# Attention in a hybrid decoder block: the softmax sums of three of four query blocks go through DRAM, and the first block's scores stand in four slots in a row

## The chip, the cores and the metric

The kernel runs on one core of a Trainium2 chip. The metric is the device time of one execution in microseconds. Before the change the median of three runs was 2093.01 us (2092.22 to 2093.68). One further execution was profiled: it took 2091.41 us, of which 2089.6 us lie between its first and its last instruction (the span that all times inside the trace are counted in). The granted TensorE clock was 0.998 of full speed over the span.

## The reference, cut to what matters

The program is one decoder block over 2048 positions with a model width of 1024: a normed input projection, eight attention heads and a gated linear recurrence side by side, an output projection, and a gate at the end. The change touches the attention alone:

```
s = einsum('bhqd,bhkd->bhqk', qi, k) * scale
s = s + (ci[:, :, :, None] - c[:, :, None, :])       # c: cumulated log sigmoid of a forget logit
s = where(kpos[None, :] <= qpos[:, None], s, -inf)
w = softmax(s, axis=-1)
o = einsum('bhqk,bhkd->bhqd', w, v)
```

The softmax divides by a sum for each query. The kernel multiplies the finished output by the reciprocal of that sum, and it is this factor, one number for each of 512 queries, that has to reach every partition of a transposed output tile.

## The kernel before, in words

**Stages.** The first 1058 us are the projections and the recurrence, then comes the attention (1058 to 1608 us), then the output projection and the gate. Products are made in three parts by `mm3`, lines 67 to 69: high times high, high times low, low times high, in a four-byte type whose operands are split in two.

**Attention.** A unit is one head and one block g of 512 queries, g = 0 to 3. Because of the causal mask unit g meets 4g+4 blocks of 128 keys. The work of 32 units is written out by hand in slots, one slot for one key block of one unit; a head has 4+8+12+16 = 40 slots. They are counted here from 0 to 39 within a head: slots 0 to 3 are block 0, 4 to 11 block 1, 12 to 23 block 2, 24 to 39 block 3. `run_slot` writes what a slot issues, and this order is the order on each engine:

1. DMAs listed for the start of the slot (the list `before`), all on the queue of SP.
2. Score pieces (`piece`, lines 1219 to 1226): three matmuls into a bank `sbank` (three of them), then one VectorE instruction that adds the bias and mask, writes the row to `pr` and reduces a running minimum `m`.
3. The value products of the slot three earlier (`AHEAD` = 3, `add_values`), into `obank`.
4. At a unit's last value product, `finish_unit`: VectorE multiplies `obank` by the spread reciprocal `rb` to give `on`.
5. `turn_probs`: up to four TensorE transposes (line 1258) of 128x128 into a bank `tbank` (three of them), which ScalarE copies as the high part `th` (line 53) and VectorE completes with the low part `tl` (line 59). At a unit's second slot `spread_sums` follows (lines 1275 to 1279): each of the four columns of the reciprocals `r4` is repeated 128 times and transposed, so that one bank holds all 512 factors on all partitions, and ScalarE copies it to `rb`.
6. `gate_unit` on VectorE (`gs`), then the exponentials of score rows that became complete in this slot (ScalarE, line 1231, with a read of the accumulated sum), then chores listed for the slot's end (the list `after`): splits of the next head's keys and values (`kh`, `vh` on ScalarE, `kl`, `vl` on GpSimd), masks, and pieces of work for the recurrence and for later weights on GpSimd.

**Where the scores of a unit stand.** They are made during the unit before it, `LEAD` = 3 slots earlier than that unit's own slots. The table `s_at` spreads the 4g+4 pieces evenly: block 1 has two pieces in a slot (slots 37 to 0), block 2 three in two slots (1 to 8), block 3 four in three slots (9 to 20), and block 0 of the next head four pieces in sixteen slots, at slots 21, 25, 29 and 33. Its pieces have 128, 256, 384 and 512 keys, and each is a complete row, so that an exponential follows each.

Of the kernel before, what the change touches and what calls it, by code (L numbers as in the profile page):

```python
# [9 lines left out]
F32 = mybir.dt.float32  # L10
F32R = mybir.dt.float32r
AF = mybir.ActivationFunctionType
# [4 lines left out]
P = 128  # L17
S = 2048
D = 1024
NH = 8  # L20
# [52 lines left out]
def hymba_kernel(ctx: ExitStack, tc: tile.TileContext, x, xT, pT, w_p, w_v, w_o, w_ple, w_pg,  # L73
                 w_gates, vecs, rows, mgrp, out):
    nc = tc.nc
    const = ctx.enter_context(tc.tile_pool(name="const", bufs=1))
    dram = ctx.enter_context(tc.tile_pool(name="dram", bufs=1, space=DRAM))
# [14 lines left out]
    vo_d = dram.tile([2, 7, 2, P, 2 * WS], F32, name="vo_d")  # L92
    yl2_d = dram.tile([TB, P, D], F32, name="yl2_d")
    rl_d = dram.tile([1, S], F32, name="rl_d")
    wt_d = dram.tile([4, P, KD, 512], F32, name="wt_d")
    p2_d = dram.tile([2, 4, P, 512], F32, name="p2_d")
    p4_d = dram.tile([2, 4, P, 512], F32, name="p4_d")
# [17 lines left out]
    ident = const.tile([P, P], F32, name="ident")  # L115
# [45 lines left out]
    def pool_(stack, name, bufs=1, side="left", space=None):  # L161
        kw = {"side": side} if space is None else {"side": side, "space": space}
        return stack.enter_context(tc.tile_pool(name=name, bufs=bufs, reuse_waits="tile", **kw))
# [728 lines left out]
    for i in range(8):  # L892
        h, c = jobs.pop(0)
# [6 lines left out]
    for n in range(2):  # L900
# [6 lines left out]
        t = 139 + 6 * n  # L907
# [14 lines left out]
    for i in range(24):  # L922
        h, c = jobs.pop(0)
        t = VB + 11 + 5 * i
# [157 lines left out]
    for m, n in enumerate((0, "q0", 1, 2, "q1", 3, 4, 5, 6, 7)):  # L1082
        t = LWE + 1 + m
# [114 lines left out]
    av = pool_(p2, "av", 2)  # L1198
# [4 lines left out]
    psT = pool_(p2s, "psT", PS // 10 % 10, space=PSUM)  # L1203
# [49 lines left out]
    def turn_probs(g, u, sb):  # L1253

        q0 = max(0, sb - 4 * g)
        b = psT.tile([P, 512], F32, name="tbank")
        for i in range(q0, 4):
            nc.tensor.transpose(b[:, i * P:(i + 1) * P], u.P[i][:, sb * P:(sb + 1) * P], ident)  # L1258
        th = av.tile([P, 512], F32R, name="th", bufs=THB)
        tl = av.tile([P, 512], F32R, name="tl", bufs=THB)  # L1260
        n = slice(q0 * P, 512)
        split(nc, b[:, n], th[:, n], tl[:, n], "act", "dve")
        u.parts[sb] = (th, tl, n)

    def add_values(h, g, u, sb):
        s = heads[h]
        nsb = 4 * g + 4
        if sb == 0:
            u.o = psO.tile([P, 512], F32, name="obank")
        th, tl, n = u.parts.pop(sb)  # L1270
        mm3(nc, u.o[:, n], (s.vh[:, sb], s.vl[:, sb]), (th[:, n], tl[:, n]), sb == 0, sb == nsb - 1)

    def spread_sums(u):

        b = psT.tile([P, 512], F32, name="tbank")
        for i in range(4):
            nc.tensor.transpose(b[:, i * P:(i + 1) * P], u.r4[:, i:i + 1].broadcast_to([P, P]), ident)
        u.rb = av.tile([P, 512], F32, name="rb")
        nc.scalar.activation(u.rb, b, AF.Copy)

    def finish_unit(h, g, u):
        u.on = av.tile([P, 512], F32, name="on")
        nc.vector.tensor_tensor(out=u.on, in0=u.o, in1=u.rb, op=ALU.mult)

    def gate_unit(u):
        nc.vector.tensor_tensor(out=u.gs, in0=u.on, in1=u.gs, op=ALU.mult)

    def add_squares(h, g, u):
        on = u.on
        cs = slice(g * 512, (g + 1) * 512)  # L1290
        eng = nc.vector if (h, g) == (NH - 1, 3) else nc.gpsimd
        if h == 0:
            nc.gpsimd.tensor_tensor(out=acca[:, cs], in0=on, in1=on, op=ALU.mult)
        else:
            eng.tensor_tensor(out=on, in0=on, in1=on, op=ALU.mult)
            eng.tensor_tensor(out=acca[:, cs], in0=acca[:, cs], in1=on, op=ALU.add)
# [5 lines left out]
    def store_y(h, g, u):  # L1302
        nc.sync.dma_start(out=ya_d[h, :, g * 512:(g + 1) * 512], in_=u.gs)

    stages = [(h, g) for h in range(NH) for g in range(4)]
    NS = len(stages)
    t0, t = [], 4
# [4 lines left out]
    units = {0: u0}  # L1312
    before = {}
    after = {}

    def at(d, slot, f):
        d.setdefault(max(slot, 0), []).append(f)

    s_at = {}
    for n, (h, g) in enumerate(stages):  # L1320
        cnt = 4 * g + 4
        if n == 0:
            continue
        begin = max(t0[n - 1] - LEAD, 0)
        span = t0[n] - LEAD - begin
        for j in range(cnt):
            s_at.setdefault(begin + j * span // cnt, []).append((n, j))

    def begin_unit(n):
        h, g = stages[n]  # L1330
        u = units[n]
        u.parts = {}
        u.units = score_units(h, g, u)
# [98 lines left out]
    def run_slot(t, fill=None):  # L1432
        for f in before.pop(t, ()):
            f()
        post = []
        for n, j in s_at.pop(t, ()):
            if j == 0:
                begin_unit(n)
            f, a, z = units[n].units[j]
            e = f(a, z)  # L1440
            if e is not None:
                post.append(e)
        if fill is not None:
            fill()
        done = None
        if t - AHEAD in slots:
            n, sb = slots[t - AHEAD]
            h, g = stages[n]
            add_values(h, g, units[n], sb)
            if sb == 4 * g + 3:  # L1450
                done = units.pop(n)
                finish_unit(h, g, done)
                at(after, t + 3, lambda: add_squares(h, g, done))
                at(before, t + 4, lambda: store_y(h, g, done))
        if t in slots:
            n, sb = slots[t]
            turn_probs(stages[n][1], units[n], sb)
            if sb == 1:
                spread_sums(units[n])
        if done is not None:  # L1460
            gate_unit(done)
        for e in post:
            e()
        if t + 1 in t0[:NS]:
            r4 = units[t0.index(t + 1)].r4
            nc.vector.reciprocal(r4, r4)
        for f in after.pop(t, ()):
            f()
# [13 lines left out]
    for t in range(last_t0 + 1):  # L1482
        run_slot(t)
# [53 lines left out]
    def fill():  # L1537
        q, ks = fills.pop(0)
        products(q, ks, bank3)
        if ks[1] == KD - 1:  # L1540
            evict(q, av.tile([P, 512], F32, name="mx", tag="th", bufs=THB))
# [6 lines left out]
    for t in range(last_t0 + 1, end):  # L1548
        run_slot(t, fill if last_t0 + 3 <= t < last_t0 + 19 else None)
    for t in sorted(set(before) | set(after)):  # L1550
        run_slot(t)
# [359 lines left out]
```

## Time and profile before

| | |
|---|---|
| median of three runs | 2093.01 us |
| the profiled execution | 2091.41 us |
| its span | 2089.6 us |
| TensorE busy over the span | 99% |
| VectorE, ScalarE, GpSimd busy | 78%, 55%, 34% |
| attention, from the first transpose of probabilities to the last value product | 1058 to 1608 us |
| spread of the sums: transposes (line 1277) | 128, 19.2 us busy |
| spread of the sums: copies (line 1279) | 32, 18.9 us busy |

In the timelines below a row gives the start and the duration in us, the engine, the line, the operation, out<-in by the program's names, and in brackets the idle time of the engine before it with what ended it. Matmuls overlap: the recorded duration of one is longer than the distance to the start of the next, so costs on TensorE are read from starts. PEld is its weight load, SPq the queue on which SP issues DMAs.

### The profile page before, as it was taken

How to read it: one execution, taken by the hardware profiler on the slowest of the kernel's cores; microseconds unless marked ns; L12 is line 12 of the kernel's file. 1: busy time of each engine (PE TensorE's matmuls, PEld its weight loads, DVE VectorE, ACT ScalarE, POOL GpSimd, SP SyncE). 2: the span in 40 equal slices, each digit the busy share in tenths (PEclk: the TensorE clock that was granted, in tenths of full speed). 3: DMA queues.
4: the chain of work that ended last, by engine and by line, in shares of the span. 5: the costliest groups of instructions: out<-in, count | busy, mean ns of one | idle time of the engine just before them, and what ended most of it. 6: DMA issues, size and time to landing. Idle time of an engine off the chain costs nothing.

```text
span 2089.6 us, 31351 instructions
## 1 busy us (share of the span) xinstructions
PE 2062.3 (99%) x10586; PEld 1744.5 (83%) x10586; DVE 1625.5 (78%) x2706; ACT 1143.7 (55%) x1871; POOL 705.5 (34%) x613
## 2 busy tenths in 40 slices
PE   8999999999999999999999999999999999999999
PEld 6888888888988898888878888888888888888887
DVE  7976998696759877895588888888885778876665
ACT  7435765344337776664367777777773443452232
POOL 3434555332113335632035665666641000000000
PEclk9999999999999999999999999999999999999999
DMA  8698898987888898888657777777744887565553
GB/s 315 211 339 300 308 347 305 368 320 285 281 275 275 277 273 290 270 296 261 242 191 236 234 221 216 235 227 241 196 148 130 283 255 227 184 216 181 179 173 119
DMA packets 256976, 518.89 MB, mean 248 GB/s; under 512 B 25120, under 2 KB 91952, under 8 KB 256816
## 3 DMA queue, kind: packets, MB, share of 16 engines
q1 hardware_dynamic: 256672, 516.85, 75.2%
q8 instruction: 83, 1.36, 0.3%
q14 instruction: 77, 0.63, 0.1%
q10 hardware_dynamic: 144, 0.05, 0.0%
HBM read 314.55 MB, written 202.25 MB: 247 GB/s over the span
## 4 chain that ended last, share of the span: by engine, by line
PE 92%; DVE 4%; DMA 2%; ACT 1%; issue 1%; SPq 0%; DVEq 0%; ACTq 0%
PE bank L69 15%; PE bank L67 15%; PE bank L68 15%; PE pbank L69 7%; PE pbank L67 7%; PE pbank L68 7%; PE tbank L1258 5%; PE sbank L67 3%; PE sbank L69 3%; PE sbank L68 3%; PE obank L68 3%; PE obank L69 3%; PE obank L67 3%; DVE pr L1222 1%; PE bank L1780 1%
## 5 line engine op out<-in xcount | busy, mean ns | idle before, releaser
L67 PE MATMUL bank<-XH,op 128*128 128x512 f32 x876 | 342.3, 391 | 0.0
L69 PE MATMUL bank<-XH,op 128*128 128x512 f32 x876 | 340.9, 389 | 0.0
L68 PE MATMUL bank<-XL,op 128*128 128x512 f32 x876 | 340.8, 389 | 0.0
L357 DVE TENSOR_TENSOR c<-bank,c 128x512 f32<-128x512 f32 x280 | 186.7, 684 | 115.3 <-PE bank L69 103.0
L59 DVE TENSOR_TENSOR tl<-tbank,th 128x512 fp32r<-128x512 f32 (+1 forms) x320 | 192.3, 607 | 82.6 <-ACT th L53 79.8
L53 ACT ACTIVATE th<-tbank 128x512 fp32r<-128x512 f32 (+1 forms) x320 | 167.6, 530 | 117.5 <-PE tbank L1258 109.8
L68 PEld LDWEIGHTS bank<-XL,op 128*128 128x128 f32 x876 | 164.5, 188 | 34.5 <-issue 0.5
L69 PEld LDWEIGHTS bank<-XH,op 128*128 128x128 f32 x876 | 164.5, 188 | 34.3
L67 PEld LDWEIGHTS bank<-XH,op 128*128 128x128 f32 x876 | 164.5, 188 | 34.0 <-issue 0.5
L1231 ACT ACTIVATE pr<-pr,m 128x640 f32<-128x640 f32 (+7 forms) x124 | 152.0, 1226 | 45.0 <-DVE m L1222 44.3
L1258 PE MATMUL tbank<-ident,pr 128*128 128x128 f32 x1088 | 171.9, 273 | 0.0
L1258 PEld LDWEIGHTS tbank<-ident,pr 128*128 128x128 f32 x1088 | 134.1, 141 | 28.2 <-issue 0.2
L150 POOL TENSOR_TENSOR rsm<-rs,mhalf 128x1 f32<-128x1 f32 x16 | 8.7, 541 | 431.5 <-DVE rs L149 431.5
L67 PE MATMUL sbank<-kh,qh 128*128 128x512 f32 (+3 forms) x320 | 136.5, 427 | 5.1 <-DVE m L1222 3.7
L67 PE MATMUL obank<-th,vh 128*128 128x512 f32 (+1 forms) x320 | 123.2, 385 | 0.8 <-ACT th L53 0.8
L284 ACT ACTIVATE op<-wq 128x512 fp32r<-128x512 f32 (+1 forms) x96 | 60.0, 629 | 110.5 <-PE bank L69 73.0
L68 PE MATMUL obank<-tl,vh 128*128 128x512 f32 (+1 forms) x320 | 117.9, 368 | 1.2 <-DVE tl L59 1.1
L69 PE MATMUL sbank<-kh,ql 128*128 128x512 f32 (+3 forms) x320 | 116.7, 365 | 0.3 <-DVE ql L1162 0.2
L69 PE MATMUL obank<-th,vl 128*128 128x512 f32 (+1 forms) x320 | 116.8, 365 | 0.0
L68 PE MATMUL sbank<-kl,qh 128*128 128x512 f32 (+3 forms) x320 | 115.8, 362 | 0.0
L68 PE MATMUL bank<-op,XH 128*128 128x258 f32 x328 | 94.9, 289 | 2.8 <-DVE op L290 2.8
L69 PE MATMUL bank<-op,XL 128*128 128x258 f32 x328 | 95.9, 292 | 0.0
(327 smaller groups left out, 5755.9 us busy)
## 6 DMA issues: line engine op xcount, KB each, us to landing
wo_d<-op SPq DMA_DIRECT2D x140, 512.0 KB, 5.3
op<-wo_d SPq DMA_DIRECT2D x79, 512.0 KB, 5.4
wr<-wo_d SPq DMA_DIRECT2D x61, 512.0 KB, 5.4
wq<-in_w_p_dram SPq DMA_DIRECT2D x40, 512.0 KB, 6.2
vo_d<-op SPq DMA_DIRECT2D x28, 516.0 KB, 3.6
wst<-wt_d SPq DMA_DIRECT2D x56, 256.0 KB, 3.5
wst<-in_w_o_dram SPq DMA_DIRECT2D x40, 256.0 KB, 3.3
X<-xr_d SPq DMA_DIRECT2D x32, 257.5 KB, 4.0
```

The costliest lines, as they stand in the source:

```text
L53: nc.scalar.activation(hi, src, AF.Copy)
L59: eng.tensor_tensor(out=lo, in0=src, in1=f32(hi), op=ALU.subtract)
L67: nc.tensor.matmul(out, lhsT=wh, rhs=xh, start=start, stop=False)
L68: nc.tensor.matmul(out, lhsT=wh, rhs=xl, start=False, stop=False)
L69: nc.tensor.matmul(out, lhsT=wl, rhs=xh, start=False, stop=stop)
L150: nc.gpsimd.tensor_tensor(out=o, in0=t, in1=mhalf[:, :n], op=ALU.pow)
L284: nc.scalar.activation(op[:, :n], self.source(i, hf), AF.Copy)
L357: nc.vector.tensor_tensor(out=o, in0=x, in1=y, op=ALU.add)
L1222: nc.vector.tensor_tensor_reduce(out=pr[0][:, a:z], in0=b[:, :z - a], in1=u.dg[i][1] if z == L else u.bias[:, a:z], scale=-1.0, scalar=BIG ...
L1231: nc.scalar.activation(pr[0][:, :L], pr[0][:, :L], AF.Exp, bias=m2, scale=-1.0, accum_out=u.r4[:, i:i + 1])
L1258: nc.tensor.transpose(b[:, i * P:(i + 1) * P], u.P[i][:, sb * P:(sb + 1) * P], ident)
L1780: nc.tensor.transpose(b[:, k * P:(k + 1) * P], u.xt[:, kk * P:(kk + 1) * P], ident)
```

## The change

**Sums.** Blocks 1, 2 and 3 of a head (24 units) no longer use `spread_sums`. In the unit's second slot one transpose turns the 128x4 tile of reciprocals into 4x128, ScalarE copies these four rows to `rr`, two slots later SP stores them to DRAM as one row of 512, and another two slots later SP loads that row to all 128 partitions of `rb`. Block 0 keeps the four transposes.

**Scores.** For block 0 of heads 1 to 7 the span over which its four pieces are spread is 4 slots in place of 16: slots 21, 22, 23 and 24 of the head before.

```diff
+    rb_d = dram.tile([NH, 4, 512], F32, name="rb_d")
...
+    def turn_sums(u):
+        b = psT.tile([P, 512], F32, name="tbank")
+        nc.tensor.transpose(b[:4, :P], u.r4, ident)
+        u.rr = av.tile([P, P], F32, name="rr")
+        nc.scalar.activation(u.rr[:4], b[:4, :P], AF.Copy)
+
+    def store_sums(h, g, u):
+        nc.sync.dma_start(out=rb_d[h, g:g + 1, :].rearrange("o (t p) -> (o t) p", p=P), in_=u.rr[:4])
+
+    def load_sums(h, g, u):
+        u.rb = av.tile([P, 512], F32, name="rb")
+        nc.sync.dma_start(out=u.rb, in_=rb_d[h, g:g + 1, :].broadcast_to([P, 512]))
...
         begin = max(t0[n - 1] - LEAD, 0)
         span = t0[n] - LEAD - begin
+        if h > 0 and g == 0:
+            span = cnt
         for j in range(cnt):
             s_at.setdefault(begin + j * span // cnt, []).append((n, j))
...
             if sb == 1:
-                spread_sums(units[n])
+                h, g = stages[n]
+                u = units[n]
+                if g == 0:
+                    spread_sums(u)
+                else:
+                    turn_sums(u)
+                    at(before, t + 2, lambda: store_sums(h, g, u))
+                    at(before, t + 4, lambda: load_sums(h, g, u))
```

ScalarE in slots 20 to 27 of head 2, before. `pr` is a row of probabilities (its width tells which: 2048 is the last row of block 3, 128 to 512 are the rows of the next head's block 0), `th` the high part of a transposed block, `kh` the split of the next head's keys:

```order
L1231 ACTIVATE pr,r_12283<-pr,m 128x2048
L53 ACTIVATE th<-tbank 128x384
L1231 ACTIVATE pr,r_12586<-pr,m 128x128
L53 ACTIVATE th<-tbank 128x256
L53 ACTIVATE th<-tbank 128x128
L53 ACTIVATE th<-tbank 128x512 x2
L1279 ACTIVATE rb<-tbank 128x512
L1231 ACTIVATE pr,r_12586<-pr,m 128x256
L53 ACTIVATE th<-tbank 128x512
L53 ACTIVATE kh<-kvf 128x512
```

The same place on ScalarE now:

```order
L1232 ACTIVATE pr,r_12284<-pr,m 128x2048
L53 ACTIVATE th<-tbank 128x384
L1232 ACTIVATE pr,r_12587<-pr,m 128x128
L53 ACTIVATE th<-tbank 128x256
L1232 ACTIVATE pr,r_12587<-pr,m 128x256
L53 ACTIVATE th<-tbank 128x128
L1232 ACTIVATE pr,r_12587<-pr,m 128x384
L53 ACTIVATE th<-tbank 128x512
L1232 ACTIVATE pr,r_12587<-pr,m 128x512
L53 ACTIVATE th<-tbank 128x512
L1286 ACTIVATE rr<-tbank 4x128
L53 ACTIVATE th<-tbank 128x512
```

The exponentials of 256, 384 and 512 columns moved from slots 25, 29 and 33 to stand between the copies `th` of slots 22 to 25, and the copy of the spread sums became one of four rows.

SP's queue around slots 25 to 32 of head 2, before. `bias` and `dg` are the biases of the next head's block 1, `kvf` its keys and values (`kT_d`, `v_d`), `yl_d` a chore of the recurrence, `ya_d` the attention's output:

```order
L1394 DMA yl_d<-kvs 128x4x128
L1147 DMA bias<-nb_d 128x512
L1153 DMA dg_12734<-nb_d 128x256
L1153 DMA dg_12736<-nb_d 128x256
L1153 DMA dg_12738<-nb_d 128x384
L1153 DMA dg_12740<-nb_d 128x512
L1110 DMA kvf<-v_d 128x512
L1303 DMA ya_d<-gs 128x512
```

The same place on SP's queue now:

```order
L1410 DMA yl_d<-kvs 128x4x128
L1289 DMA rb_d<-rr 4x128
L1148 DMA bias<-nb_d 128x512
L1154 DMA dg_12749<-nb_d 128x256
L1154 DMA dg_12751<-nb_d 128x256
L1154 DMA dg_12753<-nb_d 128x384
L1154 DMA dg_12755<-nb_d 128x512
L1111 DMA kvf<-v_d 128x512
L1293 DMA rb<-rb_d 128x512
L1317 DMA ya_d<-gs 128x512
```

The store of the four rows stands ahead of the biases and the values, and the load of the row behind them, ahead of the output's store.

## The prediction

> **What bounds the kernel now.** I read the page first, then busy time by stretches of one head, then the chain of waits where it leaves TensorE.
>
> ```profile
> PE 2062.3 (99%) x10586; PEld 1744.5 (83%) x10586; DVE 1625.5 (78%) x2706; ACT 1143.7 (55%) x1871; POOL 705.5 (34%) x613
> ```
>
> ```profile
> 1197.90:1206.30 8.40, 8.40 (x52) 7.14 (x51) 8.05 (x21) 5.68 (x9) 5.55 (x7) 1.00 0.87 275
> ...
> 1213.70:1221.00 7.30, 7.30 (x49) 6.42 (x48) 6.01 (x16) 5.47 (x9) 3.00 (x2) 1.00 0.68 208
> ```
>
> TensorE sets the time: it is 99% busy. The stretches (from:to, length, then busy time of PE, PEld, DVE, ACT and POOL, clock, DMA share, GB/s) are slots 5 to 8 and 13 to 16 of head 2. VectorE is 8.05 of 8.40 us busy in the first and 6.01 of 7.30 in the second: time taken from TensorE in slot 13 has room behind it, in slot 5 hardly any. In slots 21 to 24 TensorE itself waits; the chain of waits (start, length, what) shows on whom:
>
> ```profile
> 1231.50 0.19 ACT pr L1231
> 1231.69 0.39 ACT th L53
> 1232.11 0.57 DVE tl L59
> 1232.72 0.44 PE obank L68
> ```
>
> The value products of slot 24 need `th` and `tl` of slot 21. That `th` stands on ScalarE behind the exponential of the last row of block 3, 2048 columns wide, and slots 22 and 23 give TensorE too little work to cover it.
>
> **The sums.** Per unit four transposes become one. TensorE's timeline:
>
> ```profile
> 1234.33 0.60 PE L1258 MATMUL tbank<-ident,pr 128*128 128x128 f32 x4
> 1234.76 0.60 PE L1277 MATMUL tbank<-ident,r 128*128 128x128 f32 x4
> 1235.12 0.31 PE L67 MATMUL obank<-th,vh 128*128 128x128 f32 x1
> ...
> 1068.58 0.62 PE L1258 MATMUL tbank<-ident,pr 128*128 128x128 f32 x4
> 1069.04 0.27 PE L1376 MATMUL tbank<-ident,rstd_l 128*16 128x128 f32 x1
> 1069.07 0.48 PE L67 MATMUL sbank<-kh,qh 128*128 128x512 f32 x1
> ```
>
> Eight transposes take 1235.12 - 1234.33 = 0.79 us; four and a narrow one (16 columns, the nearest row to the new one of 4) take 1069.07 - 1068.58 = 0.49. That is 0.30 saved; the spacing inside a group is 0.43 / 4 = 0.11, and three of those are 0.33. I take 0.33, since the two groups start behind different matmuls. In 24 units that is 7.9 us of TensorE work. How much of it arrives differs by slot.
>
> *Slot 13 (block 2), eight times:* VectorE has 1.3 us of room, so all of it: 8 x 0.33 = 2.6 us. *Slot 5 (block 1), eight times:* between 0 (VectorE is the bound) and 2.6; with VectorE at 96% I take about a quarter, 0.7. *Slot 25 (block 3):* in heads 0 to 6 it is counted with the next part. In the last head no scores follow, and there I count nothing; at most it is 0.3.
>
> ScalarE's copy shrinks too; TensorE's work covers it before and after, and a slower copy would show only where `th` is late, which the next part follows.
>
> **The scores.** The three moved pieces cost TensorE and VectorE what they cost before, in another place. What changes is the waiting. The place of the wait on TensorE:
>
> ```profile
> 1231.88 0.27 PE L1258 MATMUL tbank<-ident,pr 128*128 128x128 f32 x1
> 1232.13 0.44 PE L67 MATMUL obank<-th,vh 128*128 128x384 f32 x1
> 1232.72 0.44 PE L68 MATMUL obank<-tl,vh 128*128 128x384 f32 x1 [0.15 <-DVE tl L59]
> 1233.00 0.34 PE L69 MATMUL obank<-th,vl 128*128 128x384 f32 x1
> 1233.17 0.60 PE L1258 MATMUL tbank<-ident,pr 128*128 128x128 f32 x4
> ```
>
> The last of the three products takes 0.17 us from start to start, so three and a transpose of 0.11 should take 0.62; they take 1233.17 - 1231.88 = 1.29. The wait is some 0.65 us per head. The moved pieces have 256 + 384 + 512 = 1152 columns in three products each, by 0.17 us for 384 columns some 1.5 us of work that now stands ahead of these products. So this wait goes: in seven heads 4.5 us.
>
> What is late next? The exponentials now stand between the copies `th`. The rows of ScalarE, of VectorE and of GpSimd near this place, and `gs` over all 32 units (min/median/max in ns):
>
> ```profile
> 1232.35 0.54 ACT L53 ACTIVATE th<-tbank 128x256 fp32r<-128x256 f32 x2
> ...
> 1235.93 0.51 ACT L1231 ACTIVATE pr<-pr,m 128x256 f32<-128x256 f32 x1
> ...
> 1241.16 0.62 ACT L1231 ACTIVATE pr<-pr,m 128x384 f32<-128x384 f32 x1 [0.48 <-DVE m L1222]
> ```
>
> ```profile
> 1236.20 0.68 DVE L1283 TENSOR_TENSOR on<-obank,rb 128x512 f32<-128x512 f32 x1
> 1237.06 0.69 DVE L59 TENSOR_TENSOR tl<-tbank,th 128x512 fp32r<-128x512 f32 x1 [0.18 <-ACT th L53]
> 1237.66 1.79 DVE L1286 TENSOR_TENSOR gs<-on,gs 128x512 f32<-128x512 f32 x1
> 1239.38 1.27 DVE L59 TENSOR_TENSOR tl<-tbank,th 128x512 fp32r<-128x512 f32 x2
> ```
>
> ```profile
> 1237.62 1.28 POOL L59 TENSOR_TENSOR kl<-kvf,kh 128x512 fp32r<-128x512 f32 x1 [7.23 <-ACT kh L53]
> ```
>
> ```profile
> L1286 DVE TENSOR_TENSOR gs<-on,gs x32: 680/694/1790, 1070.6 to 1608.5; 128x512 f32<-128x512 f32 x32
> ```
>
> With these durations I go through head 2 by hand, on this trace's clock. ScalarE reaches `th` of slot 22 at 1232.35 as before. The 256-column exponential waits for its minimum, which VectorE makes after `tl` of slot 21, and starts near 1233.0; `th` 23 follows at 1233.5, the 384 columns at 1234.0, `th` 24 at 1234.7, the 512 columns (0.73, the step of 0.11 added to 0.62) at 1235.2, `th` 25 at 1235.9 and `th` 26 at 1236.5. VectorE follows with `tl` 25 to 1237.2, `on` to 1237.8, `tl` 26 to 1238.4, and then comes `gs`. GpSimd's `kl`, released by a copy on ScalarE, holds from about 1237.7 to 1239.0. Beside such a `kl` the row above has `gs` at 1.79 us where the median is 0.69: it ended about half a microsecond after `kl` did. I let it end at 1239.7 and `tl` 27 at 1240.3. TensorE, 0.65 + 0.33 us ahead of its old times, wants `tl` 27 for the value products of slot 30 at about 1239.9: a new wait of some 0.45 us. The head gains 0.65 + 0.33 - 0.45 = 0.5 us, and seven heads 3.7. Bounds per head: 1.0 where `gs` isn't held up, and 0 where ScalarE and VectorE run another half microsecond late.
>
> [...]
>
> **The DMAs.** 24 stores of 2 KB and 24 broadcasts of 256 KB, 6 MB, join SP's queue. The nearest rows are the one round trip of this kind that the kernel makes already (KB, us to landing), the old copy to `rb` and its reader in block 1 of head 2, and a wait on a load, which the list of waits (us in total, times, longest) has once in the whole attention:
>
> ```profile
> pr<-rl_d SPq DMA_DIRECT2D x4, 256.0 KB, 7.4
> ...
> rl_d<-pr SPq DMA_DIRECT2D x1, 8.0 KB, 1.3
> ```
>
> ```profile
> 1201.86 0.58 ACT L1279 ACTIVATE rb<-tbank 128x512 f32<-128x512 f32 x1
> ...
> 1217.42 0.69 DVE L1283 TENSOR_TENSOR on<-obank,rb 128x512 f32<-128x512 f32 x1
> ...
> 1247.66 0.63 ACT L53 ACTIVATE vh<-kvf 128x512 fp32r<-128x512 f32 x1 [0.82 <-DMA kvf<-v_d]
> ```
>
> ```profile
> ACT vh L53 <- DMA kvf<-v_d: 0.8, 1, 0.8
> ```
>
> Block 1 is the tightest: 1217.42 - 1201.86 = 15.6 us from copy to reader. A store between 1.3 and, behind a full queue, 7.4 us, and a load of 7.4, make 8.7 to 14.8: in time, so the round trip costs 0 by itself. But SP issues in order. Its store waits for ScalarE's `rr`, its load for the store's landing, and the next queries, keys, values and biases stand behind. They come some 2 to 4 us later than now; in head 2 ScalarE already waited 0.82 us for a load of values. With three slots of lead on TensorE I count 0, and keep the loss as a rival.
>
> **The sum.** 2.6 + 0.7 + 3.7 = 7.0 us: the profiled span of 2089.6 goes to 2082.6, the profiled execution (2091.4) to 2084.4. The median of the runs lies 1.6 above the profiled execution, so I predict 2093.0 - 7.0 = 2086.0.
>
> **Rivals.** *Full gain (0.16).* All 7.9 us of transposes and the whole 0.65 in seven heads, with no new wait: 12.4 us, 2080.6. For it: TensorE is the only engine at 99%. Against it: slot 5 and the hand-made timeline. *Covered elsewhere (0.22).* ScalarE's new queue of exponentials eats the moved part and slot 25, VectorE eats slot 5; only slot 13 is left, 2.6 us: 2090.4. For it: the bounds of 0 above. *Slower: SP's queue (0.12).* In slots 27 to 29 the store holds back the biases and the next values, and ScalarE, in order, waits for the values with every `th` behind it. From about 3 us of delay TensorE's lead is used up, and each further microsecond costs one in each of seven heads: 5 us of delay cost 14 us, and with the 7 us that are gained elsewhere that makes 2100. For it: the wait of 0.82; against it: other heads show none. That the change isn't carried out as said is excluded by the order of the instructions.
>
> **Chances.** The forecast has 0.50. A measurement of this kernel tells 0.2%, 4.2 us, from no change. Faster than that: the full gain and nine tenths of the forecast, 0.61. The same: the rest of the forecast and the case covered elsewhere, 0.27. Slower: 0.12. The range goes from the full gain, 2080.5, to just under no change, 2092.5, which leaves out the slower case and a little below.
>
> **What would show it.** Right: the three products of slot 24 no longer wait; a wait of TensorE on `tl` around slot 30 in heads 0 to 6, near 0.45 us; slot 13 shorter by 0.33 us in each head; TensorE's groups of lines 1258 and 1284 at 0.49 us together. Wrong: `on` waiting for a DMA into `rb`, ScalarE waiting for `kvf` in more than one head, or stretches of slots 5 to 8 shorter by the full 0.33.

## The result: slower by 16 us, and the profile after

The changed kernel took 2108.89 us (median of four runs, 2107.90 to 2109.79), the kernel before, run beside it, 2092.61 us (2091.76 to 2093.68). The ratio is 1.0074 with a 95% interval from 1.0061 to 1.0087. The forecast was 2086.0, in a range from 2080.5 to 2092.5. The profiled execution after took 2109.74 us with a span of 2107.9 us, 18.3 more than before. The attention itself, from its first transposes to its last slot, accounts for 16.2 of them (544.0 to 560.2 us). The other 2.1 lie ahead of it, where both kernels hold the same work: over the profiles of this study the attention starts between 1057.7 and 1061.3 us.

The page's line of busy time still names TensorE, and only its share gives the loss away:

```profile
PE 2061.3 (98%) x10514; PEld 1733.5 (82%) x10514; DVE 1630.4 (77%) x2706; ACT 1137.9 (54%) x1871; POOL 704.0 (33%) x613
```

The 72 transposes are gone (10586 to 10514 matmuls), but the span grew. Where it grew is read by stretches of one head. Here is head 4 before: slots 17 to 20, 21 to 36, 37 to 40 and 1 to 4 of the next head (slot 40 is slot 0 of the next head). The columns are those of the prediction's second fence.

```profile
1354.44:1362.25 7.81, 7.81 (x47) 6.59 (x45) 6.84 (x17) 4.82 (x7) 6.20 (x8) 1.00 0.52 179
1362.25:1381.93 19.68, 19.53 (x126) 16.49 (x124) 14.28 (x30) 15.27 (x32) 12.39 (x13) 1.00 0.82 227
1381.93:1390.18 8.25, 8.25 (x50) 7.15 (x48) 6.86 (x20) 6.17 (x13) 5.54 (x6) 1.00 0.72 213
1390.18:1397.80 7.62, 7.26 (x47) 6.06 (x45) 7.18 (x18) 5.16 (x11) 4.55 (x6) 1.00 0.84 290
```

The same stretches after, with slots 13 to 16 as the first row:

```profile
1359.15:1366.17 7.02, 7.02 (x47) 6.13 (x46) 6.02 (x13) 5.51 (x11) 2.55 (x2) 1.00 0.72 229
1366.17:1374.36 8.19, 8.12 (x46) 6.53 (x45) 7.61 (x18) 4.79 (x7) 6.57 (x8) 1.00 0.53 187
1374.36:1393.86 19.50, 19.05 (x122) 16.18 (x121) 14.08 (x30) 15.29 (x32) 11.58 (x11) 1.00 0.76 220
1393.86:1403.63 9.77, 8.53 (x50) 7.09 (x48) 6.53 (x20) 5.86 (x13) 5.66 (x7) 1.00 0.76 278
1403.63:1411.69 8.06, 7.54 (x48) 6.07 (x46) 7.62 (x18) 5.27 (x12) 5.18 (x7) 1.00 0.78 277
```

Slots 13 to 16 shrank as forecast. Slots 17 to 20 grew by 0.38 us, and VectorE is busier in them by 0.77. Slots 21 to 36, where the scores moved, are 0.18 shorter. In slots 37 to 40 TensorE lost 1.5 us, and it was idle for 1.2 of 9.77.

The lengths over all heads, cut at the same matmuls, are in this table (mean of heads 0 to 6 in us, worked out from the starts of the matmuls of each trace; slots 9 to 12 hardly differ and are left out, and the last column is a whole head of 40 slots). The kernels below the second row are the experiments of the next section.

| kernel | 1 to 4 | 5 to 8 | 13 to 16 | 17 to 20 | 21 to 36 | 37 to 40 | head |
|---|---|---|---|---|---|---|---|
| before | 7.18 | 8.55 | 7.36 | 7.81 | 19.69 | 8.27 | 66.34 |
| the change | 7.91 | 8.41 | 7.02 | 8.19 | 19.50 | 10.05 | 68.61 |
| sums only | 7.72 | 8.39 | 7.02 | 8.19 | 19.36 | 9.59 | 67.81 |
| scores only | 6.99 | 8.40 | 7.36 | 7.81 | 19.50 | 8.27 | 65.72 |
| loads only | 7.55 | 8.26 | 7.02 | 8.19 | 19.50 | 8.37 | 66.34 |
| blocks 1 and 2 | 7.31 | 8.31 | 7.02 | 8.18 | 19.52 | 8.58 | 66.44 |
| store later | 7.47 | 8.31 | 7.08 | 8.34 | 19.51 | 8.44 | 66.65 |
| store of constants | 7.77 | 8.26 | 7.05 | 8.20 | 19.51 | 9.05 | 67.32 |

So the loss has two places. Slots 37 to 40 and 1 to 4 cost 1.78 + 0.73 = 2.51 us in each head, 17.6 us in seven. Slots 17 to 20 cost 0.38, which eats the 0.34 of slots 13 to 16.

**The first place: late keys and values.** The list of waits inside the attention (us in total, times, longest) had one wait of ScalarE for a load before. After, it has two in each of seven heads:

```profile
ACT kh L53 <- DMA kvf<-kT_d: 18.1, 7, 3.4
ACT vh L53 <- DMA kvf<-v_d: 13.1, 7, 3.4
```

SP's own waits, the first two of the list, stand on the new instructions:

```profile
SPq L1289 <- ACT rr L1286: 46.5, 13, 5.2
SPq L1293 <- DMA rb_d<-rr: 35.7, 14, 5.0
```

By units they divide: of the first, 28.8 us stand at block 3's store in heads 0 to 6. The second, the wait of a load for its store's landing, stands at blocks 1 and 2 and in head 7; block 3's load in heads 0 to 6 waits 0.5 us at most.

How the one leads to the other is seen in head 4. First SP before, from the biases of the next unit to the load of keys:

```profile
1365.54 0.38 SPq L1147 DMA_DIRECT2D bias<-nb_d  x1
1365.97 3.69 SPq L1153 DMA_DIRECT2D dg<-nb_d  x4
1372.34 0.32 SPq L1110 DMA_DIRECT2D kvf<-v_d  x1
...
1375.30 0.32 SPq L1108 DMA_DIRECT2D kvf<-kT_d  x1
```

Then SP after, and ScalarE where it takes these loads up:

```profile
1378.04 1.68 SPq L1427 DMA_DIRECT2D wt_d<-qh  x1
1382.30 0.26 SPq L1289 DMA_DIRECT2D rb_d<-rr  x1
1382.65 0.32 SPq L1148 DMA_DIRECT2D bias<-nb_d  x1
1383.02 1.85 SPq L1154 DMA_DIRECT2D dg<-nb_d  x4
1384.99 0.36 SPq L1111 DMA_DIRECT2D kvf<-v_d  x1
...
1386.87 1.62 SPq L1293 DMA_DIRECT2D rb<-rb_d  x1
...
1390.17 0.69 SPq L1109 DMA_DIRECT2D kvf<-kT_d  x1
```

```profile
1392.42 0.63 ACT L53 ACTIVATE vh<-kvf 128x512 fp32r<-128x512 f32 x1 [1.06 <-DMA kvf<-v_d]
1392.96 1.78 ACT L53 ACTIVATE th<-tbank 128x512 fp32r<-128x512 f32 x3
1397.66 0.63 ACT L53 ACTIVATE kh<-kvf 128x512 fp32r<-128x512 f32 x1 [2.91 <-DMA kvf<-kT_d]
```

Slot 25 starts at 1366.94 before and at 1380.00 after, which makes the two comparable. Before, SP had the biases out 1.4 us ahead of slot 25: it runs ahead of the other engines. After, SP stands 2.6 us at the store (1379.72 to 1382.30), and the biases leave 2.65 us behind the start of slot 25. The load of values leaves at about its old place (5.0 us behind, 5.4 before), but with a bias and four masks directly ahead of it. ScalarE, which waits for it, takes it up at 1392.4, 7.4 us later; before, the record of its landing gives 5.2. The load of keys leaves 10.2 us behind in place of 8.4, past the broadcast, and takes 7.5 us in place of 4.9. The same holds in the other heads: the biases leave 2.7 us behind the start of slot 25 in all of heads 0 to 6 after, and 1.4 to 2.0 us ahead of it before, but for head 2, where they left 1.3 us behind and ScalarE waited already. ScalarE waits 1.06 and 2.91 us with three `th` behind it, VectorE's `tl` and minima follow late, and TensorE's scores stand for want of a free bank:

```profile
1399.92 0.45 PE L67 MATMUL sbank<-kh,qh 128*128 128x384 f32 x1 [1.24 <-DVE m L1223]
```

**The second place: `gs` of block 1.** Before, in head 2: ScalarE's copy of the sums and the split behind it, GpSimd's two products, VectorE's `gs`.

```profile
1216.27 0.59 ACT L1279 ACTIVATE rb<-tbank 128x512 f32<-128x512 f32 x1
1216.75 0.63 ACT L53 ACTIVATE kh<-kvf 128x512 fp32r<-128x512 f32 x1
...
1217.46 1.30 POOL L59 TENSOR_TENSOR kl<-kvf,kh 128x512 fp32r<-128x512 f32 x1 [7.64 <-ACT kh L53]
1218.72 1.74 POOL L1391 TENSOR_TENSOR kvs<-kvs,pr 128x512 f32<-128x512 f32 x1
...
1218.62 0.69 DVE L1286 TENSOR_TENSOR gs<-on,gs 128x512 f32<-128x512 f32 x1
```

The same rows after, in head 2:

```profile
1223.22 0.25 ACT L1286 ACTIVATE rr<-tbank 4x128 f32<-4x128 f32 x1
1223.38 0.61 ACT L53 ACTIVATE kh<-kvf 128x512 fp32r<-128x512 f32 x1
...
1224.07 1.31 POOL L59 TENSOR_TENSOR kl<-kvf,kh 128x512 fp32r<-128x512 f32 x1 [6.68 <-ACT kh L53]
1225.33 1.30 POOL L1407 TENSOR_TENSOR kvs<-kvs,pr 128x512 f32<-128x512 f32 x1
...
1225.57 1.60 DVE L1300 TENSOR_TENSOR gs<-on,gs 128x512 f32<-128x512 f32 x1
```

Before, `gs` started 0.10 us ahead of `kvs`: it took 0.69, and `kvs` took 1.74. After, `kvs` started 0.24 ahead: it took 1.30, and `gs` took 1.60. In both, the one that starts first takes its usual time (0.69 and 1.30 are also the medians of the 32 `gs` and of the 32 `kvs` before), and the other 0.44 or 0.91 us more than its own. ScalarE's copy of the sums is what swapped them. It takes 0.25 in place of 0.59, so `kh` follows 0.16 us behind its start and not 0.48, GpSimd is earlier by that, and VectorE is not. This holds in heads 0 to 6, in which `gs` of block 1 took 1.54 to 1.61 us; before, it started 0.03 to 0.10 us ahead of GpSimd's product in all of them and took 0.68 to 0.69. Block 2 before shows the same the other way round: in heads 0 to 6 `kl` starts 0.05 us ahead of `gs` and takes 1.28 to 1.29 us, and `gs` takes 1.79.

### The profile page after: what moved, and what is told of

Same layout as the page of the kernel before. It is cut to its first block, busy times and chain, and to the rows that moved or that the text cites. A ratio compares the mean times of both kernels' runs of the same rounds, so it can differ in the third digit from the quotient of the medians.

```text
span 2107.9 us, 31263 instructions
## 1 busy us (share of the span) xinstructions
PE 2061.3 (98%) x10514; PEld 1733.5 (82%) x10514; DVE 1630.4 (77%) x2706; ACT 1137.9 (54%) x1871; POOL 704.0 (33%) x613
```

## The experiments

Ratios are to the kernel before, run on the same chip beside each group (medians 2091.6 to 2092.5 us), with their 95% intervals. Each edit is against the change unless it says otherwise. The first four take the change apart.

**Sums only: the scores stay spread.**

```diff
-        if h > 0 and g == 0:
-            span = cnt
```

> Only the sums go by DRAM; the scores of the first block stay spread over sixteen slots. Three theories of the 16 us that the change lost. A, order on SP's queue: the store of block 3's sums stands on SP until ScalarE has made rr, and the next loads of values and keys stand behind it; ScalarE then waits for them. B, traffic: the 24 broadcasts of 256 KB make every load land later, wherever they stand. C, crowding: the exponentials of four slots in a row make ScalarE and VectorE late, and the sums have nothing to do with it. Here no exponentials of the next head stand ahead of rr in slots 21 to 24, so that store should wait about 1 us and not 2.5 to 5.3. A: 2089 to 2096, with waits of ScalarE for kvf under 10 us in all (31 in the changed kernel). B: 2104 or more. C: 2089, and no wait for kvf.

Measured: 2103.27 us, ratio 1.0051 [1.0036, 1.0066]; ScalarE waits 21.2 us for `kvf`. By its time alone this is nearest to B, which the run with loads only, below, rules out. Theory A had the right place and a wrong picture. No exponentials stand ahead of `rr` here, yet block 3's store still waits 1.3 to 4.3 us in heads 0 to 6, because SP gets to it so early. C falls as the main cause: without the moved scores most of the loss is there.

**Scores only: all sums by four transposes.**

```diff
-                if g == 0:
+                if True:
                     spread_sums(u)
```

> Only the scores move into four slots; all sums by four transposes on TensorE as before, no new DMA. A and B: the prediction's term for the scores stands by itself, 2092.6 - 3.7 = 2089 (2087 to 2092), ScalarE waits for kvf about as before (0.8 us in all). C: slower than before, 2100 or more.

Measured: 2090.08 us, ratio 0.9986 [0.9977, 0.9996]. The scores by themselves gain: a head takes 65.72 us in place of 66.34. That excludes C. ScalarE's waits for `kvf` are 2.3 us in all, against 0.8 before.

**Loads only: no stores, the broadcasts read a row that is already in DRAM.**

```diff
-                    at(before, t + 2, lambda: store_sums(h, g, u))
...
-        nc.sync.dma_start(out=u.rb, in_=rb_d[h, g:g + 1, :].broadcast_to([P, 512]))
+        nc.sync.dma_start(out=u.rb, in_=qT_d[h, g:g + 1, :512].broadcast_to([P, 512]))
```

> The change with its 24 stores left out; the 24 broadcasts of 256 KB stay at their places but read a row of the queries that has lain in DRAM since long before, so nothing on SP waits for rr or for a landing (the multiplier of the output is then another, so the result is not the reference's). The traffic is the same but for 48 KB. A: the loss is gone, 2083 to 2089. B: as the change, 2104 or more. C: as the change, 2104 or more.

Measured: 2093.31 us, ratio 1.0001 [0.9991, 1.0012]. The loss is gone with the waits, and the traffic stayed, so B is not the main cause. But it is 4 us above what A allowed at most. Of this, slots 1 to 4 are 0.56 us longer than with the scores alone, and slots 17 to 20 are at 8.19, so `gs` collides here too.

**Blocks 1 and 2 by DRAM, block 3 as before.**

```diff
-                if g == 0:
+                if g in (0, 3):
                     spread_sums(u)
```

> The change with block 3's sums by four transposes as before; blocks 1 and 2 still go by DRAM, 16 of the 24 round trips. A: their stores wait too (up to 4.3 us), but at slots 7 and 15, where the next loads of keys and values have 5 us of margin or more, so the loss is gone: 2087 to 2090. B: two thirds of the traffic stay, 2098 or more. C: as the change, 2104 or more.

Measured: 2094.29 us, ratio 1.0008 [0.9997, 1.0018]. Without block 3's round trip slots 37 to 40 fall from 10.05 to 8.58. Most of the loss is that one round trip in seven heads. The 4 to 7 us that are missing against A are again in slots 17 to 20 (0.37 a head longer than with the scores alone), 1 to 4 (0.32) and 37 to 40 (0.31, from heads 2 and 4 alone).

**Three variants of block 3's store.** First its place: three slots later, and the load five, behind the loads of values that had stood behind it.

```diff
-                    at(before, t + 2, lambda: store_sums(h, g, u))
-                    at(before, t + 4, lambda: load_sums(h, g, u))
+                    at(before, t + (5 if g == 3 else 2), lambda: store_sums(h, g, u))
+                    at(before, t + (9 if g == 3 else 4), lambda: load_sums(h, g, u))
```

> The change with block 3's store three slots and its load five slots later on SP (slots 30 and 34), so behind the load of values of slot 29; blocks 1 and 2 as in the change. A: rr is long made when SP comes to the store, the waits for kvf fall to what the kernel with blocks 1 and 2 alone has (5 us), and slots 37 to 40 go back from 10.05 to about 8.5 us: 2090 to 2096. Rival, traffic at that place: the broadcast of 256 KB ahead of the next loads keeps them late, 2100 or more.

Measured: 2092.86 us, ratio 1.0000 [0.9990, 1.0009]. Slots 37 to 40 are at 8.44, and ScalarE's waits are down to:

```profile
ACT vh L53 <- DMA kvf<-v_d: 3.8, 2, 2.0
ACT kh L53 <- DMA kvf<-kT_d: 2.8, 2, 1.7
```

The same transfers, in another order on SP, cost 16 us less. Next, the wait for `rr` alone: the store stays at its place and stores a tile that is always ready.

```diff
-... .rearrange("o (t p) -> (o t) p", p=P), in_=u.rr[:4])
+... .rearrange("o (t p) -> (o t) p", p=P), in_=ident[:4])
```

> The change with its stores at their places, but from a tile of constants that has lain ready since the start, so that the store waits for no rr; the copy to rr is still made, the load of rb still waits for the store's landing (the multiplier of the output is another, so the result is not the reference's). A, the wait for rr: slots 37 to 40 back from 10.05 to 8.3 to 8.7 us, waits of ScalarE for kvf under 8 us, 2090 to 2096. Rival, the landing: the load's wait for the store, at slots 9, 17 and 29, takes over; 2100 or more.

Measured: 2097.72 us, ratio 1.0032 [1.0018, 1.0046], between the two forecasts. ScalarE's waits fall from 31.2 to 13.3 us:

```profile
ACT vh L53 <- DMA kvf<-v_d: 7.9, 5, 2.6
ACT kh L53 <- DMA kvf<-kT_d: 5.4, 4, 3.3
```

So the wait for `rr` by itself makes more than half of the loss: 11 of 16 us by the medians, 1.29 of 2.27 us by the length of a head. What is left at block 3 is not the landing. SP's waits at the loads, for the store's landing, are 51.0 us in all, against 35.7, but they stand at blocks 1 and 2 and in head 7; block 3's load in heads 0 to 6 waits 0.2 us at most. Slots 37 to 40 are at 8.25 to 8.28 in five of the seven heads, as before the change; the rest of the loss there is head 2 (9.39) and head 4 (12.67). In these two SP has the biases out 0.9 and 2.2 us behind the start of slot 25, with no store to wait for. This run also shows how far SP runs ahead: with nothing to wait for, the store written for slot 27 leaves in slots 23 to 26.

The third variant gives the 24 stores to ScalarE, which makes `rr` itself.

```diff
+        nc.scalar.dma_start(out=rb_d[h, g:g + 1, :].rearrange("o (t p) -> (o t) p", p=P), in_=u.rr[:4])
...
-                    at(before, t + 2, lambda: store_sums(h, g, u))
```

> The change with its 24 stores issued by ScalarE, right behind the copy that makes rr, so that nothing on SP waits for rr; the loads of rb stay on SP at their places, and the result is the change's. A, order on SP's queue: the waits of ScalarE for kvf go (31 us in the changed kernel, under 6 here) and the kernel lands where the one without stores landed, 2089 to 2095. Rival, the round trip itself: the loads' wait for the store's landing (36 us on SP in the changed kernel) is what holds the queue; then most of the loss stays, 2100 or more.

Measured: 2113.11 us, ratio 1.0104 [1.0086, 1.0121], slower than the change. As A says, slots 37 to 40 are back at 8.36, and ScalarE's waits for `kvf` at 3.4 us. But the loss came back in other slots, up to 13.2 us for slots 13 to 16 in head 3. ScalarE there:

```profile
1289.82 0.25 ACT L1286 ACTIVATE rr<-tbank 4x128 f32<-4x128 f32 x1
1297.20 0.25 ACTq L1287 DMA_DIRECT2D rb_d<-rr  x1
1297.55 0.63 ACT L53 ACTIVATE kh<-kvf 128x512 fp32r<-128x512 f32 x1 [7.48 <-DMA dg<-nb_d]
```

The store itself waited 7.1 us (from the copy's end at 1290.07 to 1297.20), and every `th` behind it. It waited for a mask load that has nothing to do with it: the last row puts the end of the idle time down to a landing of `dg`. In the records each transfer names one of eight semaphores in rotation (all 1498 of them in the trace before), and the one of this store is that of the mask load of 1287.16, eight transfers earlier. That part of the wait is for that landing, not for the round trip, so this run does not test the rival cleanly for the whole time; what it shows is a third way to lose the same time. For block 3 it speaks against the rival: SP's waits for the landing grew to 69.6 us in all, and slots 37 to 40 did not suffer.

The run also shows what swapped `gs` and GpSimd's product. ScalarE's issue of the store stands between the copy and `kh`, which comes 0.57 us or more behind the copy's start again. `gs` of block 1 starts 0.2 us ahead of GpSimd's product in heads 0 to 6 and takes 0.77 to 0.80 us, the product 1.72 to 1.77, and slots 17 to 20 are at 7.83 to 7.85 in six of the seven heads.

**The collision of `gs`.** VectorE's `gs` one slot later in the program, which nothing near needs:

```diff
         if done is not None:
-            gate_unit(done)
+            at(after, t + 1, lambda: gate_unit(done))
```

On the kernel with ScalarE's stores:

> As the kernel with ScalarE's stores, and VectorE's gs of every unit stands one slot later in its order. Theory D, collision: gs of block 1 takes 1.5 to 1.6 us in every head of the kernels with DRAM sums (0.69 before), since ScalarE's shorter copy lets GpSimd's next product start ahead of it; that makes slots 17 to 20 0.38 us longer and eats slot 13's gain; and gs of block 2 beside the product kl makes the wait of slot 30, 0.45. A slot later both products are through: 7 x (0.38 + 0.45) = 5.8 us less than the kernel with ScalarE's stores alone. Rival: the collision only moves to another slot, and the time stays within 2 us of it.

Measured: 2113.52 us, ratio 1.0097 [1.0082, 1.0111]; a head is 0.2 us shorter. The first of D's two terms, 0.38 for block 1, was not there to be won: its `gs` is not held in the kernel with ScalarE's stores. The stalls at these stores move from slot to slot (slots 17 to 20 went from 8.04 to 9.00), and nothing can be told of the second term. On the scores alone:

> Only the scores move, sums as before, and gs one slot later. D: the wait of slot 30 (0.45 us in seven heads) goes, 3.2 us less than the scores alone: some 2086 to 2087. Rival, the collision only moves: as the scores alone, 2089 to 2090.

Measured: 2087.93 us, ratio 0.9979 [0.9969, 0.9989]. `gs` over its 32 units, with the scores alone and then with `gs` later (min/median/max in ns):

```profile
L1300 DVE TENSOR_TENSOR gs<-on,gs x32: 680/693/1781, 1071.4 to 1605.6; 128x512 f32<-128x512 f32 x32
```

```profile
L1300 DVE TENSOR_TENSOR gs<-on,gs x32: 676/684/1444, 1075.4 to 1606.1; 128x512 f32<-128x512 f32 x32
```

Units with over 0.9 us fall from 13 to 3, and slots 29 to 32 from 4.98 to 4.51 us. The whole wait of slot 30 is gone; some of it comes back in slots 33 to 36 (0.14) and 1 to 4 (0.13), so 1.9 us and not 3.2 arrive in heads 0 to 6. The intervals of the two ratios overlap; it is the slots of the traces that tell the two kernels apart. On the change itself:

> The change as it is, stores and loads at its places, with gs one slot later. If the two causes stand side by side: slots 17 to 20 back from 8.19 to 7.83 and slots 29 to 32 from 4.95 to 4.51 in every head, 0.8 x 7 = 5.6 us, 2103. Rival: the wait in slots 37 to 44 takes up what is won ahead of it, since the late loads set when those slots can run: 2107 or more.

Measured: 2104.18 us, ratio 1.0061 [1.0045, 1.0077]. Slots 17 to 20 are at 7.89 and slots 29 to 32 at 4.51, as expected. Slots 37 to 40 grew from 10.05 to 10.72, most of it in head 2 (10.24 to 13.89), so a part is given back. That ScalarE comes earlier to loads that are as late as before would explain it, but is not shown. On the kernel before:

> The kernel before with nothing but gs one slot later. By the collision theory as told, gs beside GpSimd's product costs TensorE nothing there, since no wait of slot 30 exists and block 1's gs is free: 2091 to 2093. Rival, gs held up costs in other slots too: 2089 or less.

Measured: 2089.35 us, ratio 0.9987 [0.9979, 0.9996]. The rival was nearer: a `gs` that is held costs TensorE something without the moved scores too. Slots 5 to 8 fall from 8.55 to 8.27, and the `gs` of block 0, which stands there, from 1.25 to 0.75 us (mean of heads 0 to 6). The move itself, without a hold, gave nothing where it can be seen alone: block 1's `gs` takes 0.69 in both kernels, and slots 13 to 20 keep their length (7.36 and 7.37, 7.81 and 7.81).

**Repaired versions.** With `gs` later, the scores moved and the round trips spaced out, for one block, two and three (the blocks left out keep `spread_sums`):

```diff
-                    at(before, t + 2, lambda: store_sums(h, g, u))
-                    at(before, t + 4, lambda: load_sums(h, g, u))
+                    at(before, t + (2, 2, 2, 5)[g], lambda: store_sums(h, g, u))
+                    at(before, t + (4, 5, 6, 9)[g], lambda: load_sums(h, g, u))
```

> Scores moved, gs one slot later, and only block 2's sums (8 of 32) by DRAM: store at slot 15, load at slot 19, two slots later than in the change, so that SP does not stand at the load until the store has landed. If slot 13's gain of 0.33 us is kept once gs does not collide: 2.6 us less than the scores with the later gs (2087.9), so 2085 to 2086. Rival, every added transfer costs the queue what TensorE gains: 2088 or more.

> As the kernel with block 2 alone, and block 1's sums by DRAM too (store at slot 7, load at slot 10). If only the wait of block 3's store and the collision of gs made the change slow: another 0.33 us in eight heads less, 2083. Rival, the queue: block 1's round trip makes the masks and biases of slots 37 to 44 late, as in the kernel with blocks 1 and 2 by DRAM (slots 1 to 4 0.3 us and slots 37 to 40 0.3 us longer than with the scores alone): 2087 or more.

> The whole change with its round trips spaced (store and load at slots 7 and 10, 15 and 19, 30 and 34) and gs one slot later. If the two causes are all there is: slot 25's 0.33 us is eaten in slot 26 by the wait for ScalarE, so as the kernel with blocks 1 and 2, 2083. Rival, the queue: above it by what the third round trip costs, 2088 to 2092.

Measured: block 2 alone 2085.70 us, ratio 0.9972 [0.9961, 0.9983]; blocks 1 and 2 2085.93, 0.9971 [0.9960, 0.9982]; all three 2087.70, 0.9984 [0.9975, 0.9993]. The forecast for block 2 held; the second came out between its two forecasts, and the third just short of its rival. The whole change, in another order and with `gs` out of the way, is slightly faster than the kernel before and not slower. Block 2 keeps slot 13's gain (slots 13 to 16 at 7.02, slots 17 to 20 at 7.84). Block 1 gains 0.21 us in slots 5 to 8 and gives 0.13 back in slots 37 to 40. Block 3 wins nothing: a head takes 65.68 us with it and 65.16 without, though more than half of that difference is one stretch, slots 17 to 20 of head 4 (9.96 against 7.83), where `gs` was held once more for 1.77 us. By their intervals the three cannot be told from one another.

## Why the prediction was wrong, point by point

- **The step that failed: "With three slots of lead on TensorE I count 0" for the DMAs.** The prediction named the chain that happened, as its rival on SP's queue, and gave it 0.12. Block 3's store waited 2.5 to 5.3 us in each of heads 0 to 6, and ScalarE for the next keys and values 4.5 us per head. Of this, 2.5 us per head arrived in slots 37 to 40 and 1 to 4, 17.6 us in all; 2.1 of the 2.5 go when block 3's round trip alone is left out (10.05 and 7.91 fall to 8.58 and 7.31), the rest stands with blocks 1 and 2. So the lead took up 2.0 to 2.4 of ScalarE's 4.5. The rival's price of 2100 was too low for two reasons. It counted 7 us of gain elsewhere, of which some 2 came. And it let the loss begin at 3 us of delay, where the lead covered 2.0 to 2.4. The argument against it, that other heads showed no wait, was weak: by the records of before the tighter of the two loads had 1.5 to 3.0 us of margin in six heads, and 0.02 in head 2.
- **"Its store waits for ScalarE's `rr`"** was taken as a delay of 2 to 4 us of what stands behind it. The load of values did not leave later in its slot. The biases and masks did, 4 us later in head 4, and the values right behind them took 2.2 us longer. The keys, the larger part of ScalarE's wait (18.1 of 31.2 us), left 1.8 us later there and took 2.6 us longer.
- **Why SP waits.** The prediction reasoned in slots as if SP came to the store at slot 27. The store of constants leaves in slots 23 to 26, in six of heads 0 to 6 ahead of slot 25, which makes `rr`: the wait was built in.
- **Slot 13, 2.6 us.** The transposes' 0.33 is right to 0.01 (7.36 to 7.02). It did not arrive, because "TensorE's work covers" the shorter copy on ScalarE was wrong: the copy pulled GpSimd ahead of `gs`, and slots 17 to 20 lost 0.38. With `gs` one slot later, or with `kh` put back behind ScalarE's store, that loss is gone (7.81 to 7.85 in six of seven heads of either kernel).
- **Slot 5, 0.7 us.** About the full 0.33 arrives where nothing else disturbs (head 0 from 8.33 to 8.00; elsewhere 8.07 to 8.14 us in five heads with loads only, against 8.39 to 8.48 in heads 1 to 6 with scores only). VectorE at 96% was no bound. In the change the mean of heads 0 to 6 gained 0.14, 1.0 us in all, near the term, but as the full gain less new stalls.
- **Slot 25, counted as 0.33 in seven heads.** It went one slot further. With scores and sums both changed, TensorE stands at the transposes of slot 26 for a bank that ScalarE and VectorE have yet to empty:

```profile
1242.64 0.27 PE L1284 MATMUL tbank<-ident,r 128*4 128x128 f32 x1
...
1243.49 0.66 PE L1259 MATMUL tbank<-ident,pr 128*128 128x128 f32 x4 [0.28 <-DVE tl L59]
```

  With the sums alone slots 21 to 36 gain the 0.33 (19.69 to 19.36).
- **The scores.** The mechanism and both sizes were right. The 0.65 at slot 24 went, and a new wait of 0.45 appeared at slot 30, for `tl` behind the `gs` that took 1.54 us beside GpSimd's `kl`. TensorE after, the products of slot 24, then those of slots 29 and 30:

```profile
1240.89 0.33 PE L67 MATMUL obank<-th,vh 128*128 128x384 f32 x1
1241.06 0.34 PE L68 MATMUL obank<-tl,vh 128*128 128x384 f32 x1
1241.24 0.34 PE L69 MATMUL obank<-th,vl 128*128 128x384 f32 x1
...
1246.16 0.47 PE L67 MATMUL obank<-th,vh 128*128 128x512 f32 x1
1246.47 0.39 PE L68 MATMUL obank<-tl,vh 128*128 128x512 f32 x1
1246.69 0.40 PE L69 MATMUL obank<-th,vl 128*128 128x512 f32 x1
...
1247.28 0.47 PE L67 MATMUL obank<-th,vh 128*128 128x512 f32 x1
1247.93 0.50 PE L68 MATMUL obank<-tl,vh 128*128 128x512 f32 x1 [0.17 <-DVE tl L59]
1248.27 0.39 PE L69 MATMUL obank<-th,vl 128*128 128x512 f32 x1
```

  Slot 24 steps by 0.17 us throughout. In slot 30 the first two steps are 0.65 and 0.34 us where slot 29 has 0.31 and 0.22: a wait of 0.46. Net, slots 21 to 36 gained 0.19 us per head, 1.3 in seven. The term of 3.7 held 2.3 for slot 25, which leaves 1.4.
- **Its list of signs.** Of those for wrong, ScalarE waited for `kvf` in seven heads, and slots 5 to 8 fell by about the full 0.33 in the heads left undisturbed. Of those for right, slot 24, the wait near slot 30 and slot 13 came as said, and the group of lines 1259 and 1284 takes 0.46 us in 23 of 24 units (0.49 was forecast). `on` waiting for `rb`, the sign that was looked for first, did not come: the round trip was in time by itself, as worked out. It hurt by where it stood.

What stays open is the part of the loss that the store of constants keeps. It is not the landing, for which block 3's load waits 0.2 us at most there, and in slots 37 to 40 it stands in heads 2 and 4 alone. These are also the heads in which SP is late with the biases in the kernel with the store three slots later (0.5 and 0.9 us behind the start of slot 25, where the other five have them out 1.8 us ahead or more). What makes SP late in these two is not shown; block 2's load, ahead of it, waits for its landing about as long in most heads (4.2 to 5.0 us in six of the seven).

## What to carry to other kernels

A DMA that waited for a fresh result cost, in this kernel, by what stood behind it on its queue and by how far that queue ran ahead, not by its own duration: the same transfers took 2108.89 us in the order of the change and 2092.86 in another. Put such a DMA behind the loads that have little margin, at a place where its input is long made. Before counting a wait as covered, look up the margin of the next loads in every head, not only the waits that already show (here 0.02 us in head 2, 1.5 to 3.0 in six others). And shortening work on an engine off the path can shift who meets whom, as ScalarE's copy did here (0.25 us in place of 0.59, and slots 17 to 20 0.38 us longer): check the instructions that follow it for a neighbour that they collide with.

## What the runs showed of the hardware

- **In this program a transfer waits for the eighth before it.** In the trace before, none of 438 issues in the attention comes before the eighth transfer ahead of it has landed, and 70 come within 0.3 us of that landing; 123 come before the seventh ahead has landed (worked out from issue and landing of each record). Small transfers take a place as large ones do: the 24 stores of 2 KB stand in the rotation of the 1546 transfers of the trace after like the others. One of the 24 that ScalarE issued left that engine idle for 7.48 us, while 14 of them left within 0.05 us of the copy.
- **A collision decided by 0.1 us.** `gs` (0.69 alone) and `kvs` (1.30 alone) cost 0.69 and 1.74 when `gs` starts 0.10 us ahead, and 1.60 and 1.30 when `kvs` starts 0.24 ahead. By the ratios to the kernel before, moving `gs` by one slot was worth 1.5 to 3 us in three pairs of kernels, of which only the kernel before itself is clear of noise, and nothing in the fourth, with ScalarE's stores.
